# Linear attention with chained states: the products with the states split from their evacuation, and the order of a pair of heads changed

## The chip, the cores and the metric

The kernel runs on one core of a Trainium2 chip. A core has five engines with a queue each, and each queue is worked off in order: TensorE (PE, with its weight loads as PEld) multiplies matrices into PSUM, ScalarE (ACT) and VectorE (DVE) take results out of PSUM and do the elementwise work, GpSimd (POOL) and SyncE (SP) do little here but issue transfers. The metric is the device time of one execution in microseconds. A program says which data an instruction needs; semaphores make the queues wait for each other.

## The reference, cut to what matters

The trunk has two layers over 512 tokens of 1024 features: latent attention and a squared-ReLU MLP, then gated linear attention (GLA) and another MLP. The change is in the GLA mixer, which has four heads with keys of 128 and values of 256.

```
h = xn @ w_in                      # q, k: 512 columns each; v, g: 1024 each; a: 16
gk = log_sigmoid(a @ w_gk_up + b_gk) / 16
b = cumsum(gk) within a chunk
o = (q * exp(b)) @ state + (decayed q k^T, lower triangle) @ v
state = state * exp(b_last) + (k * exp(b_last - b))^T @ v
o = rms_norm(o, g_norm) * silu(g)
out = o @ w_o
```

The kernel cuts the 512 tokens into 4 tiles of 128. Within a tile it builds the decayed scores by halving levels. Between tiles it uses three chained states: state i sums what tiles 0 to i leave to tile i+1, and tile i+1 adds its decayed queries times state i.

## The kernel before, in words

All weights are float32. A product is made of three matmuls over a high and a low part of each operand (`mm3`, lines 110 to 114; `add`, line 1326, for the attention of a head). A weight piece is loaded by SP, then cut by ACT into `wh` (line 104) and by DVE into `wl` (line 107), with three buffers of each.

`gla` has a main stream, `proj()`, and a side stream, `heads()`. `proj()` makes, in this order, the values of heads 0 and 1 ("v"), their gates ("g"), the queries and the keys of heads 2 and 3 ("q", "k"), the values ("V") and the gates ("G") of heads 2 and 3. Each of v, g, V, G is 96 matmuls of 512 columns and counts 8 units; q and k count 4 units each, 48 matmuls each. So a unit is 12 matmuls, and there are 40: v is 1 to 8, g 9 to 16, q 17 to 20 (handed out in twos), k 21 to 24, V 25 to 32, G 33 to 40. After every unit the side stream is let on by 1.27 steps (`PACE`); what it has not done after unit 40 follows behind. The scheduler takes, on each engine, the instruction that stands earliest in this program order among those that are ready, and so keeps this order but for small shifts.

The side stream does heads 0 and 1, then 2 and 3. For a pair of heads it has these steps:

- twelve steps of levels, six for each head, the last of which (`turned`) cuts the decayed queries into `qd` and turns the keys (`kth`, `ktl`); a thirteenth ends the last head's (`late`).
- `states(h)`: nine matmuls of 256 columns for the three sums over a tile (PSUM tag `c`), then their chain on ACT (lines 1319 and 104) and DVE (lines 1315 and 107) into three tiles `S`. There are three buffers of `S` in all, so the next head's `S` can be written only when `past` of the head before has read its own.
- `own_tiles(h)`: twelve matmuls of a head's own scores (`ADh`, `ADl`) times its values. They open the head's two PSUM banks: tags `bb`, `bc`, `aa`, `bb` for heads 0 to 3. The projections of values and gates hold all three `b` banks, so head 3 can have its banks only when G is over; head 2 has the `a` banks, which G does not use.
- `past(h)`: nine matmuls of the queries (`qd`) times `S`, added to the same banks. In the same function stand the squares (ACT, line 1344) and the products with the gates (DVE, line 1346), which empty the banks; these need the gates after their silu (line 1053), so the step comes after `gdone`.
- `gates(2)` and `gates(3)` (once, between the first pair's): the forget gates of heads 2 and 3, from one matmul (line 1142) and a chain on ACT and DVE.
- `head_norm(h)`, and `gather(h)`: the norm, then transposes (line 129) and the cut into `Y` (lines 1365, 1366) for the output projection.

After the second pair's `head_norm`, `out_start` makes 24 matmuls of the output projection with the first pair's `Y`, ahead of the second pair's `gather`; `out_proj` goes on from there. The silu needs its own table of ACT: it is loaded before the four silus of a gate half and the exp and ln table after them.

Of the kernel before, what the change touches and what calls it, by code (L numbers as in the profile page):

```python
# [20 lines left out]
S = 512  # L21
NT = S // P
# [28 lines left out]
def trunk_kernel(ctx: ExitStack, tc: tile.TileContext, t_in: dict, out: bass.AP, out_row: bass.AP):  # L51
# [7 lines left out]
    def uname(s):  # L59
        count[0] += 1  # L60
        return f"{s}_{count[0]}"
# [14 lines left out]
    def bank(tag):  # L76
        return psum["pool"].tile([P, 512], F32, tag=f"ps_{tag}", bufs=psum["banks"][tag], name=uname("ps"))
# [11 lines left out]
    def tmp(shape=(P, 512), dt=F32):  # L89
        return sb.tile(list(shape), dt, tag="tmp", bufs=6, name=uname("tmp"))  # L90
# [30 lines left out]
    def act_e(*a, **k):  # L121
        with tc.issue_after(table[0].ins):
            return ACT.activation(*a, **k)
# [19 lines left out]
    def cut(pair, *idx):  # L143
        return tuple(t[idx] for t in pair)
# [56 lines left out]
    def gcol(name, j):  # L201
        c = GAIN_COL[name] + j
        return gains[:, c : c + 1]
# [559 lines left out]
    def out_start(w2d, X, n):  # L763
        raw = col_chunk(w2d, 0, 256)
        w = [piece(raw[:, :, j * P : (j + 1) * P], ND, P) for j in range(2)]
        ps_ = [bank("a"), bank("a")]

        def mms(ks):
            for k in ks:
                for j in range(2):  # L770
                    mm3(ps_[j], cut(w[j], slice(None), k), X[k], k == 0, k == ND - 1)

        mms(range(n))
        return ps_, lambda: mms(range(n, ND))
# [233 lines left out]
    def gla(layer, nrm, vtag, ytag):  # L1008
# [114 lines left out]
        vdone, gdone = set(), set()  # L1123
# [16 lines left out]
        def gates(h):  # L1140
            p = bank("c")
            PE.matmul(p, wg[:, h * P : (h + 1) * P], av, start=True, stop=True)
            bcol = gcol("bgk", 4 * layer + h)
            l = tmp()
            ACT.activation(l, p, AF.Abs, bias=bcol)
            m_ = tmp()
            DVE.tensor_scalar(m_, p, bcol, 0.0, ALU.add, ALU.min)
            act_e(l, l, AF.Exp, scale=-1.0)
            act_e(l, l, AF.Ln, bias=one_t)

            T = gp.tile([P, 2 * S], F32, tag="T", bufs=3, name=uname("T"))
            DVE.tensor_tensor(T[:, :S], m_, l, ALU.subtract)
            n = S
            c = 0
            D_ = {}
            while n >= 4:
                D_[S // n] = T[:, c : c + n]
                if n > 4:
                    pair_ = T[:, c : c + n].rearrange("p (n a) -> p n a", a=2)
                    DVE.tensor_tensor(T[:, c + n : c + n + n // 2], pair_[:, :, 0], pair_[:, :, 1], ALU.add)  # L1160
                c += n
                n //= 2
            act_e(T[:, :c], T[:, :c], AF.Exp, scale=GSCALE)
            B[h] = D_
# [5 lines left out]
        AT = {}  # L1170
# [131 lines left out]
        def tile_of(pair, i):  # L1302
            return cut(pair, slice(None), slice(i * P, (i + 1) * P))
# [20 lines left out]
        def add(h, i, w, x, start, stop):  # L1324
            for n, (a, b_) in enumerate(((w[0], x[0]), (w[0], x[1]), (w[1], x[0]))):
                PE.matmul(AT[h]["o"][i], a, b_, start=start and n == 0, stop=stop and n == 2, skip_group_check=True)  # L1326
# [6 lines left out]
                add(h, i, at[(i, i)], v[i], i % 2 == 0, i == 0)  # L1333

        def past(h):
            at, hf = AT[h], h // 2
            at["ms"] = sb.tile([P, NT], F32, tag="gms", bufs=2, name=uname("gms"))
            for i in range(NT):
                if i:
                    add(h, i, tile_of(at["q"], i - 1), at["S"][i - 1], False, True)  # L1340
                if i % 2:
                    for r in (i - 1, i):
                        sq = tmp((P, HV))
                        ACT.activation(sq, at["o"][r], AF.Square, accum_out=at["ms"][:, r : r + 1])
                        g = G[hf][:, r, h % 2, :]
                        DVE.tensor_tensor(g, at["o"][r], g, ALU.mult)
# [36 lines left out]
        def heads():  # L1383
            for h in (0, 2):
                while any(i not in qk for i in (h, h + 1, 4 + h, 5 + h)):
                    yield
                late = None
                for two in zip(levels(h), levels(h + 1)):
                    for stage in two:
                        products = stage()  # L1390
                        if late:
                            late()
                        late = products
                        yield
                late()
                yield
                while h // 2 not in vdone:
                    yield

                def run(*stages):  # L1400
                    for stage, r in stages:
                        stage(r)
                        yield

                yield from run((states, h), (own_tiles, h), (states, h + 1))
                while h // 2 not in gdone:
                    yield
                yield from run((own_tiles, h + 1), (past, h))
                if h == 0:
                    gates(2)  # L1410
                yield from run((past, h + 1))
                if h == 0:
                    gates(3)
                yield from run((head_norm, h), (head_norm, h + 1))
                if h:
                    begun.append(out_start(w_o, Y, 4))
                yield from run((gather, h), (gather, h + 1))
# [3 lines left out]
        for _ in rest:  # L1421
            pass
        gates(1)
        main, side = proj(), heads()
        pace = 0.0
        for units in main:
# [194 lines left out]
```

## Time and profile before

| | |
|---|---|
| median of 3 runs | 1086.43 us (1085.32 to 1087.2) |
| the profiled execution, its own time | 1086.99 us |
| its span, first to last instruction | 1085.2 us |
| mean granted TensorE clock | 0.996 |
| PE busy | 1075.3 us |
| DVE, ACT busy | 862.5 us, 555.5 us |

The GLA mixer's side stream lies between about 541 and 706 us of the span, the gate half G between 662 and 688 us with the work put into it. A timeline row gives the start in the span, the time taken, engine, line, operation, the names written and read, shapes, and how many instructions are merged in the row; a bracket at its end gives idle time of the engine before it and what ended that. A matmul's time has its pipeline in it; the distance between the starts of two tells what it costs in a row of many. A row of the stretches gives length of the stretch and, for each engine, busy time and count of instructions, then the granted clock and the DMA's share.

### The profile page before, as it was taken

How to read it: one execution, taken by the hardware profiler on the slowest of the kernel's cores; microseconds unless marked ns; L12 is line 12 of the kernel's file. 1: busy time of each engine (PE TensorE's matmuls, PEld its weight loads, DVE VectorE, ACT ScalarE, POOL GpSimd, SP SyncE). 2: the span in 40 equal slices, each digit the busy share in tenths (PEclk: the TensorE clock that was granted, in tenths of full speed). 3: DMA queues.
4: the chain of work that ended last, by engine and by line, in shares of the span. 5: the costliest groups of instructions: out<-in, count | busy, mean ns of one | idle time of the engine just before them, and what ended most of it. 6: DMA issues, size and time to landing. Idle time of an engine off the chain costs nothing.

```text
span 1085.2 us, 14051 instructions
## 1 busy us (share of the span) xinstructions
PE 1075.3 (99%) x5352; PEld 907.6 (84%) x5352; DVE 862.5 (79%) x1446; ACT 555.5 (51%) x947; POOL 43.7 (4%) x72
## 2 busy tenths in 40 slices
PE   9999999999999999999999999999999999999997
PEld 7888888888888888888788888788888888888886
DVE  7899968987887887977696596469888797797885
ACT  7767654553453453455346655656445345344454
POOL 8310002000000000000000000000000000000000
PEclk9999999999999999999999999999999999999999
DMA  7311232142332332322322213142233234223222
GB/s 225 88 50 39 79 116 78 58 137 78 117 117 78 117 117 78 107 88 79 89 76 78 78 40 117 40 152 66 93 117 117 78 92 131 89 80 124 70 97 78
DMA packets 86195, 101.61 MB, mean 94 GB/s; under 512 B 7440, under 2 KB 64016, under 8 KB 86128
## 3 DMA queue, kind: packets, MB, share of 16 engines
q1 hardware_dynamic: 84320, 99.67, 29.0%
q10 hardware_dynamic: 1808, 1.05, 0.3%
q8 instruction: 42, 0.69, 0.3%
q14 instruction: 25, 0.20, 0.1%
HBM read 98.35 MB, written 2.10 MB: 93 GB/s over the span
## 4 chain that ended last, share of the span: by engine, by line
PE 97%; DVE 1%; ACT 1%; issue 0%; DMA 0%; SPq 0%; ACTq 0%; DVEq 0%
PE ps L114 21%; PE ps L112 21%; PE ps L113 21%; PE ps L923 17%; PE ps L924 9%; PE ps L1199 1%; PE ps L129 1%; PE ps L408 1%; PE ps L871 1%; PE ps L1326 1%; PE ps L671 0%; PE ps L667 0%; PE ps L1249 0%; PE ps L670 0%; PE ps L669 0%
## 5 line engine op out<-in xcount | busy, mean ns | idle before, releaser
L112 PE MATMUL ps<-set,wh 128*128 128x512 f32 x760 | 297.5, 392 | 0.0
L113 PE MATMUL ps<-set,wh 128*128 128x512 f32 x760 | 297.3, 391 | 0.0
L114 PE MATMUL ps<-set,wl 128*128 128x512 f32 x760 | 297.0, 391 | 0.0
L104 ACT ACTIVATE wh<-wraw 128x1024 fp32r<-128x1024 f32 x139 | 147.0, 1061 | 229.1 <-PE ps L113 116.0
L107 DVE TENSOR_TENSOR wl<-wraw,wh 128x1024 fp32r<-128x1024 f32 x139 | 169.4, 1219 | 48.4 <-ACT wh L104 48.2
L114 PEld LDWEIGHTS ps<-set,wl 128*128 128x128 f32 x760 | 143.1, 188 | 30.2
L112 PEld LDWEIGHTS ps<-set,wh 128*128 128x128 f32 x760 | 142.9, 188 | 30.1
L113 PEld LDWEIGHTS ps<-set,wh 128*128 128x128 f32 x760 | 143.2, 188 | 27.6
L923 PE MATMUL ps<-T,wh 128*128 128x512 f32 x448 | 157.5, 391 | 0.0
L924 PE MATMUL ps<-T,wl 128*128 128x256 f32 x448 | 126.2, 282 | 0.0
L923 PE MATMUL ps<-set,wh 128*128 128x512 f32 x336 | 119.9, 397 | 0.0
L923 PEld LDWEIGHTS ps<-T,wh 128*128 128x128 f32 x448 | 84.1, 188 | 18.2
L924 PE MATMUL ps<-set,wl 128*128 128x256 f32 x336 | 94.2, 280 | 0.0
L107 DVE TENSOR_TENSOR wl<-comb,wh 128x1024 fp32r<-128x1024 f32 x42 | 51.3, 1222 | 46.2 <-ACT wh L104 46.0
L104 ACT ACTIVATE wh<-comb 128x1024 fp32r<-128x1024 f32 x42 | 44.6, 1061 | 83.3 <-PE ps L923 81.8
L837 DVE TENSOR_TENSOR xT<-ps,xT 128x512 f32<-128x512 f32 x120 | 82.1, 685 | 6.1 <-PE ps L114 6.1
L924 PEld LDWEIGHTS ps<-T,wl 128*128 128x128 f32 x448 | 84.6, 189 | 0.5
L923 PEld LDWEIGHTS ps<-set,wh 128*128 128x128 f32 x336 | 63.1, 188 | 15.1
L941 DVE TENSOR_TENSOR tmp<-ps,tmp 128x512 f32<-128x512 f32 x98 | 67.1, 685 | 0.9
L924 PEld LDWEIGHTS ps<-set,wl 128*128 128x128 f32 x336 | 63.4, 189 | 1.6
L104 ACT ACTIVATE wh<-raw 128x1024 fp32r<-128x1024 f32 x28 | 29.5, 1054 | 56.7 <-PE ps L923 55.8
L112 PE MATMUL ps<-wh,set 128*128 128x512 f32 x144 | 57.9, 402 | 0.0
(372 smaller groups left out, 1662.8 us busy)
## 6 DMA issues: line engine op xcount, KB each, us to landing
wraw<-in_mlp_w_up_dram SPq DMA_DIRECT2D x32, 1024.0 KB, 5.4
wraw<-in_mlp_w_down_dram SPq DMA_DIRECT2D x18, 1024.0 KB, 5.1
raw<-in_mlp_w_down_dram SPq DMA_DIRECT2D x14, 1024.0 KB, 5.1
wraw<-in_gla_w_in_dram SPq DMA_DIRECT2D x12, 1024.0 KB, 5.2
wraw<-in_mla_w_o_dram SPq DMA_DIRECT2D x4, 1024.0 KB, 5.4
wraw<-in_gla_w_o_dram SPq DMA_DIRECT2D x4, 1024.0 KB, 5.3
xT<-in_x_dram SPq DMA_DIRECT2D x6, 256.0 KB, 5.5
wraw<-in_mla_w_in_dram SPq DMA_DIRECT2D x3, 512.0 KB, 6.6
```

What stands on the lines that cost most here:

```text
L104: order(ACT.activation(hi, src, AF.Copy))
L107: lo_eng.tensor_tensor(lo, src, f(hi), ALU.subtract)
L112: PE.matmul(psum, wh, xh, start=start, stop=False)
L113: PE.matmul(psum, wh, xl, start=False, stop=False)
L114: PE.matmul(psum, wl, xh, start=False, stop=stop)
L129: PE.transpose(psum, src, ident[: src.shape[0], : src.shape[0]])
L408: PE.matmul(p, w[:, i, j * P : (j + 1) * P], x, start=start, stop=stop)
L837: DVE.tensor_tensor(xT[m], p, xT[m], ALU.add)
L871: PE.matmul(ps_[c], a, b_, start=False, stop=k == 3 and n == 2, skip_group_check=True)
L923: PE.matmul(o.rearrange("p (h t) -> p h t", h=2), wh, x, start=start and k == 0, stop=False, skip_group_check=True)
L924: PE.matmul(o[:, :TH], wl, x[:, 0], start=False, stop=k == KH - 1, skip_group_check=True)
L941: DVE.tensor_tensor(by_tile(r), high, by_tile(r), ALU.add)
```

## The change

`past` is cut into two functions: `past(h)` keeps the nine matmuls with the states, and `gated(h)` has the squares and the products with the gates. The order of the steps is written out for each pair.

For heads 0 and 1 the wait for the gates moves ahead of `states(0)`; after it come `states(0)`, `own_tiles(0)`, `states(1)`, `own_tiles(1)`, `past(0)`, `gated(0)`, then `gates(2)`, `past(1)`, `gated(1)`, and `gates(3)`. For heads 2 and 3, `past(2)` stands ahead of `states(3)` and both ahead of the wait for the gates; after the wait come `gated(2)`, `own_tiles(3)`, `past(3)`, `gated(3)`. Each pair has two steps more.

```diff
         def past(h):
+            at = AT[h]
+            for i in range(1, NT):
+                add(h, i, tile_of(at["q"], i - 1), at["S"][i - 1], False, True)
+
+        def gated(h):
             at, hf = AT[h], h // 2
             at["ms"] = sb.tile([P, NT], F32, tag="gms", bufs=2, name=uname("gms"))
             for i in range(NT):
-                if i:
-                    add(h, i, tile_of(at["q"], i - 1), at["S"][i - 1], False, True)
                 if i % 2:
                     for r in (i - 1, i):
                         sq = tmp((P, HV))
...
-                yield from run((states, h), (own_tiles, h), (states, h + 1))
-                while h // 2 not in gdone:
-                    yield
-                yield from run((own_tiles, h + 1), (past, h))
                 if h == 0:
+                    while 0 not in gdone:
+                        yield
+                    yield from run((states, 0), (own_tiles, 0), (states, 1), (own_tiles, 1), (past, 0), (gated, 0))
                     gates(2)
-                yield from run((past, h + 1))
-                if h == 0:
+                    yield from run((past, 1), (gated, 1))
                     gates(3)
+                else:
+                    yield from run((states, 2), (own_tiles, 2), (past, 2), (states, 3))
+                    while 1 not in gdone:
+                        yield
+                    yield from run((gated, 2), (own_tiles, 3), (past, 3), (gated, 3))
                 yield from run((head_norm, h), (head_norm, h + 1))
```

## The prediction, made before the changed kernel was run

> **What bounds the kernel now.** I began with the page: busy times, the granted clock, the chain that ended last.
>
> ```profile
> span 1085.2 us, 14051 instructions
> ...
> PE 1075.3 (99%) x5352; PEld 907.6 (84%) x5352; DVE 862.5 (79%) x1446; ACT 555.5 (51%) x947; POOL 43.7 (4%) x72
> ...
> PE 97%; DVE 1%; ACT 1%; issue 0%; DMA 0%; SPq 0%; ACTq 0%; DVEq 0%
> ```
>
> TensorE is the bound, and the change adds or removes no matmul. It can win only what PE loses by waiting or by a low clock, and lose only by making new waits. So the second view is who PE waited for, over the whole span; the two rows that have to do with the change are these (total, times, longest, in us).
>
> ```profile
> PE ps L1326 <- ACT S L104: 1.0, 2, 0.7
> PE ps L1326 <- DVE S L107: 0.5, 1, 0.5
> ```
>
> L1326 is `add`, so PE waits for state tiles `S` to be cut. The third view cuts the end of the GLA mixer into stretches (length, then PE, PEld, DVE, ACT, POOL busy, then the clock).
>
> ```profile
> 629.00:662.00 33.00, 33.00 (x173) 28.57 (x172) 30.80 (x75) 18.23 (x36) 0.00 (x0) 1.00 0.29 94
> 662.00:675.00 13.00, 13.00 (x74) 11.31 (x73) 6.38 (x11) 5.43 (x10) 0.00 (x0) 1.00 0.19 61
> 675.00:687.70 12.70, 12.70 (x57) 10.51 (x57) 2.45 (x2) 5.36 (x6) 0.00 (x0) 1.00 0.19 64
> 687.70:695.30 7.60, 5.91 (x34) 4.51 (x33) 4.13 (x9) 5.89 (x16) 0.00 (x0) 1.00 0.22 78
> 695.30:698.70 3.40, 3.40 (x10) 2.63 (x9) 2.95 (x12) 3.24 (x16) 0.00 (x0) 0.50 0.01 2
> ```
>
> Two things show. PE is full until 687.7, is busy for 5.91 of the next 7.60 us, and then runs at clock 0.50 for 3.4 us. And DVE is full (30.80 of 33) while the levels of heads 2 and 3 run, but idles afterwards. The fourth view is PE's timeline there.
>
> ```profile
> 665.30 0.32 PE L112 MATMUL ps<-set,kth 128*128 128x256 f32 x1
> ...
> 668.91 0.40 PE L1326 MATMUL ps<-set,ADh 128*128 128x256 f32 x2
> ...
> 670.33 0.28 PE L112 MATMUL ps<-set,kth 128*128 128x256 f32 x1
> ...
> 671.40 0.40 PE L112 MATMUL ps<-wh,set 128*128 128x512 f32 x1
> ...
> 687.74 0.40 PE L1326 MATMUL ps<-set,ADh 128*128 128x256 f32 x2
> ...
> 689.16 2.18 PE L1326 MATMUL ps<-S,qd 128*128 128x256 f32 x12
> 692.02 0.38 PE L1326 MATMUL ps<-S,qd 128*128 128x256 f32 x1 [0.69 <-ACT S L104]
> 692.92 0.50 PE L1326 MATMUL ps<-S,qd 128*128 128x256 f32 x2 [0.51 <-DVE S L107]
> 693.76 0.96 PE L1326 MATMUL ps<-S,qd 128*128 128x256 f32 x3 [0.34 <-ACT S L104]
> 694.58 0.50 PE L112 MATMUL ps<-set,wh 128*128 128x512 f32 x1
> ...
> 695.42 0.63 PE L112 MATMUL ps<-set,wh 128*128 128x512 f32 x1
> ...
> 698.79 0.39 PE L114 MATMUL ps<-set,wl 128*128 128x512 f32 x1
> ...
> 701.77 1.47 PE L129 MATMUL ps<-ident,g 128*128 128x128 f32 x12
> 703.14 0.73 PE L112 MATMUL ps<-set,wh 128*128 128x512 f32 x2
> ```
>
> Read it with the steps. 665.30 is `states(2)`, 668.91 `own_tiles(2)`, 670.33 `states(3)`, all inside the gate half G; 671.40 to 687.74 are G's last 72 matmuls, 0.227 us each. Then `own_tiles(3)`, 12 matmuls in 1.42 us (0.118 each), and from 689.16 the 18 of `past(2)` and `past(3)`. Though the products of `states(3)` were done by 671.40, their `S` are cut only now, since the three buffers of `S` are held by head 2 until `past(2)`, which stood behind G. ACT's timeline shows what that chain meets:
>
> ```profile
> 687.94 0.69 ACT L1053 ACTIVATE g<-ps,rtok 128x512 f32<-128x512 f32 x1 [0.68 <-PE ps L114]
> 688.65 1.28 ACT L119 ACT_TABLE_LOAD   x1
> 689.94 0.38 ACT L104 ACTIVATE S<-ps 128x256 fp32r<-128x256 f32 x1
> 690.22 1.05 ACT L104 ACTIVATE wh<-wraw 128x1024 fp32r<-128x1024 f32 x1
> ```
>
> The last silu and the table load hold the first cut up to 689.94, and a weight cut of 1.05 us gets in between.
>
> **The change, part by part.**
>
> *Where the steps land.* The side stream gets 1.27 steps a unit. Before, the end of the levels (`late`) is step 40, in unit 32; `states(2)` is 41 (unit 33), `own_tiles(2)` and `states(3)` 42 and 43 (unit 34); then it waits for unit 40. The trace agrees: `states(2)` comes after G's first unit. After the change heads 0 and 1 wait until unit 16 with `states(0)` (step 20, it was 14) and each pair has two steps more. Counting on: `past(0)`, `gated(0)` 24 and 25 (unit 20), `gates(2)` with `past(1)` 26 (unit 22), `gates(3)` 28 (unit 24), levels of heads 2 and 3 steps 32 to 43 (units 26 to 34), `late` 44 (35), `states(2)` 45 (36), `own_tiles(2)` 46 (37), `past(2)` and `states(3)` 47 and 48 (both unit 38), wait in 39, `gated(2)` in 40. Behind G stand `own_tiles(3)`, `past(3)`, `gated(3)`.
>
> *`past(2)` inside G.* Nine matmuls of 0.118, 1.06 us, move ahead of G's end; G ends at 687.74 + 1.06 = 688.80. That costs nothing in sum. Does it find its `S`? The chain of head 2 runs in G already:
>
> ```profile
> 666.25 0.48 ACT L1319 ACTIVATE tmp<-ps,D 128x256 f32<-128x256 f32 x1 [2.03 <-PE ps L114]
> ```
> ```profile
> 665.09 0.55 DVE L107 TENSOR_TENSOR ktl<-ps,kth 128x384 fp32r<-128x384 f32 x1
> ...
> 669.27 0.42 DVE L107 TENSOR_TENSOR S<-tmp,S 128x256 fp32r<-128x256 f32 x1 [0.15 <-ACT S L104]
> ```
>
> From 665.30, the start of the products, to 669.69 are 4.4 us. Between `states(2)` and `past(2)` will lie its own 9 matmuls (1.1), two units (24 x 0.227 = 5.4) and `own_tiles(2)` (1.4): 7.9 us. So no wait.
>
> *`states(3)` cut inside G.* Its `S` are free as soon as `past(2)` has read. After its products come units 39 and 40 (5.4 us) and `own_tiles(3)` (1.4 us), 6.8 us in all, against the chain's 4.4 - 1.1 = 3.3 us behind the products. ACT's silus fall into this stretch; the chain may have to let by a table load (1.28) and two silus (2 x 0.69), which makes 6.0 us. It still fits by 0.8 us. So the 18 matmuls from 689.16 to 694.58, 5.42 us where 18 x 0.118 = 2.13 would do, lose their wait: **-3.29 us**. (The brackets show only 1.54 us of it, since the modelled ends of matmuls count as busy.)
>
> *The clock.* The eight matmuls from 695.42 to 698.79 take 3.37 us, and at 0.227 would take 1.81. The low clock begins 0.7 us after the wait ends, and while PE has work there is no other drop in the span (stretches as above):
>
> ```profile
> 6.00:687.70 681.70, 681.19 (x3380) 573.60 (x3379) 545.79 (x971) 363.04 (x634) 41.70 (x62) 1.00 0.29 91
> ...
> 698.70:1081.00 382.30, 380.13 (x1914) 322.54 (x1913) 307.16 (x440) 179.87 (x281) 0.00 (x0) 1.00 0.30 97
> ```
>
> I take it as the wait's doing: **-1.56 us**. [...]
>
> *What is late next.* Behind G, PE has `own_tiles(3)` 1.42, `past(3)` 1.06 and the 24 matmuls of `out_start` (5.45), so it comes to `gather(2)` at 688.80 + 7.93 = 696.7 instead of 701.77, and, eight transposes of 1.37 / 12 = 0.114 later, to `gather(3)` at 697.6. The norm chain has to keep up:
>
> ```profile
> 696.25 0.38 ACT L1344 ACTIVATE tmp<-ps 128x256 f32<-128x256 f32 x1
> ...
> 696.63 0.38 ACT L1344 ACTIVATE tmp<-ps 128x256 f32<-128x256 f32 x1
> ...
> 698.07 0.19 ACT L1344 ACTIVATION_READ_ACCUMULATOR tmp<-ps 128x1 f32 x1
> ...
> 699.48 0.91 ACT L1353 ACTIVATE g<-g,srstd 128x256 f32<-128x256 f32 x2 [0.66 <-DVE srstd L285]
> ```
>
> ACT's last silu ends 0.89 us after G (688.63 - 687.74), the table load 1.28 later, at 691.0. Eight squares at 0.38 bring 694.0, the weight cut 1.05 more, 695.1; from the last square (698.26) to the last scaling (700.39) it took 2.13, so 697.2. It is in time by 0.4 us even if no square of head 2 is done earlier. This cover is thin; without it the cost is what ACT is late by, at most 1 us.
>
> *Heads 0 and 1 later.* `states(0)`, `own_tiles(0)` and `states(1)` leave the first gate half and go between q and k, which are PE work that is always at hand. `past(0)` comes two units behind, longer than the chain of 4.4 us. `past(1)` stands two units (5.4 us) behind `past(0)`, which frees its `S`: 3.3 us are needed. I cost both at nothing.
>
> *Levels of heads 2 and 3 later.* `gates(3)` moves from unit 20 to 24 (10.9 us), the levels' end from unit 32 to 35, `states(3)` from 34 to 38 (10.9 us and `past(2)`). Head 3's keys were cut at 665.64, 4.7 us before their use; that slack stays. DVE's full stretch will reach some 9 us into G, where it is idle for 6.6 of 13 and 10.2 of 12.7 us. The emptying of V's banks, which G's first matmuls need, then stands among level work. No row shows that; between nothing (no gain, for PE has no wait there to lose) and 1.5 us (some two of the longest single wait, 0.69), I take +0.35, nearer to nothing, as PE did not wait once from 629 to 687.7 under a full DVE.
>
> *Queues.* No moved step issues a transfer; SP's loads come from the main stream, whose order stays. POOL has nothing here. The added wait for the first gates holds back steps of the program, not an engine.
>
> *Sum.* -3.29 - 1.56 + 0.35 = -4.5 us. The profiled execution took 1086.99 (span 1085.2 and 1.8 around it), so it would take 1082.5; the median of the runs stands 0.56 lower, at 1086.43, which gives **1081.9 us**.
>
> **The rivals.**
>
> 1. *A unit late.* The full DVE holds head 2's keys for a unit or two, so `states(3)` runs right before G's end and its chain meets four silus and two table loads. For: the slack is 0.8 us. Against: before, the steps were on time by G. With one unit between them, the chain ends 3.3 + 2.66 - 2.7 = 3.3 us behind G, and `past(3)` would begin at 1.42: some 1.8 us of the wait stay, 1083.7.
> 2. *The clock drops all the same*, at another place or with the waits that are left. For: gaps of 0.3 to 0.7 us only brought it about, and small ones will remain. Against: it is the only drop, right behind the wait. Then 1086.43 - 3.29 + 0.35 = 1083.5.
> 3. *The change doesn't do what it says*: the chain of `states(3)` is put behind the silus on ACT, as now. Then `past(3)` waits as now, while `past(2)` no longer helps to cover it (1.06 us): between 1086.4 and 1087.5.
> 4. *Slower.* The late start of heads 0 and 1 pushes the levels through the stretch where DVE has no room, and `states(2)` falls behind G. It decides when the keys of head 2 come over four units and the work between, some 15 us, later than planned. Then two chains stand open, each of 4.4 us, less the 3.9 us of products that can go first (1.1 + 1.42 + 1.42): a stall of about 4.9 us instead of 3.29, and another window of low clock: 1088.0 to 1089.6. The same sign would come from `past(1)` or V's first matmuls waiting for head 1's banks.
>
> **How the numbers follow.** The forecast has 0.55, rival 1 0.11, rival 2 0.08, rival 3 0.09, rival 4 and its kin 0.17. The first three make faster 0.74; a change within 0.2% (2.2 us, about what a measurement of this kernel can tell from none) 0.09; slower 0.17. The range starts at 1080.8, the full -4.85 with some 0.8 for small waits on the chain behind the gather, and ends at 1086.6, which takes in rival 3's lower end and leaves out rival 4.
>
> **What would show it.** In the changed profile nine matmuls `ps<-S,qd` stand inside G, before `states(3)`; no wait of L1326 for `S` is left near 690; the clock stays 1.00 from 687 to 700; G's end is some 1 us later and the first transposes of the second pair come about 4 us earlier, without a wait for `g`. It is wrong if `S` cuts still stand behind the table load at L119, if DVE's late levels show as waits of PE for banks at the change from V to G, or if PE waits between q and k.

## The result, and the profile after

The changed kernel takes 1084.27 us (median of 8 runs, 1083.29 to 1084.92); the kernel before, run beside it, 1087.0 us (median of 8, 1085.32 to 1088.36). The ratio is 0.9974, with a 95% interval of 0.9963 to 0.9984. So 2.7 us are won (1.7 to 4.0 by the interval) where 4.5 were forecast. The profiled execution took 1084.2 us with a span of 1082.2 us, against 1086.99 and 1085.2.

The page of the changed kernel, its first lines and the shares of the chain that ended last:

```profile
span 1082.2 us, 14050 instructions
...
PE 1072.8 (99%) x5352; PEld 906.4 (84%) x5352; DVE 864.5 (80%) x1446; ACT 556.2 (51%) x947; POOL 43.7 (4%) x72
...
PE 96%; DVE 2%; ACT 1%; DMA 0%; issue 0%; SPq 0%; DVEq 0%; ACTq 0%
```

PE has the same 5352 matmuls. DVE's share of the chain has gone from 1% to 2%, but a rounded per cent is some 11 us of the span and tells nothing of a wait of one. The view of waits for PE (total, times, longest, in us) no longer has a row of L1326; two rows of this stretch are new:

```profile
PE ps L112 <- DVE g L1349: 0.8, 1, 0.8
PE ps L112 <- ACT set L1368: 0.2, 1, 0.2
```

The stretches (length, then PE, PEld, DVE, ACT, POOL busy, then the clock) answer to those of before:

```profile
662.00:675.00 13.00, 13.00 (x70) 11.07 (x70) 8.24 (x12) 8.82 (x19) 0.00 (x0) 1.00 0.50 163
675.00:689.00 14.00, 14.00 (x77) 12.14 (x76) 5.20 (x10) 7.34 (x15) 0.00 (x0) 1.00 0.23 76
689.00:692.60 3.60, 2.75 (x23) 2.51 (x21) 1.65 (x5) 3.57 (x10) 0.00 (x0) 1.00 0.00 0
692.60:698.10 5.50, 5.50 (x24) 4.48 (x25) 4.54 (x15) 4.36 (x17) 0.00 (x0) 1.00 0.01 1
```

The clock is 1.00 throughout. DVE was busy for 6.38 of 13 us from 662 to 675 and is now busy for 8.24: the levels have moved into G, as worked out. In these stretches PE is full but for one place between 689.0 and 692.6, and there ACT is full (3.57 of 3.60). PE's timeline:

```profile
681.46 1.22 PE L1326 MATMUL ps<-S,qd 128*128 128x256 f32 x9
682.51 0.28 PE L112 MATMUL ps<-set,kth 128*128 128x256 f32 x1
...
683.58 0.39 PE L112 MATMUL ps<-wh,set 128*128 128x512 f32 x1
...
689.03 0.40 PE L1326 MATMUL ps<-set,ADh 128*128 128x256 f32 x2
...
690.45 1.22 PE L1326 MATMUL ps<-S,qd 128*128 128x256 f32 x9
692.52 0.51 PE L112 MATMUL ps<-set,wh 128*128 128x512 f32 x1 [0.85 <-DVE g L1349]
...
698.11 1.70 PE L129 MATMUL ps<-ident,g 128*128 128x128 f32 x12
700.05 0.73 PE L112 MATMUL ps<-set,wh 128*128 128x512 f32 x2 [0.25 <-ACT set L1368]
```

`past(2)` (681.46) stands inside G, without a wait, and `states(3)` (682.51) behind it. G's last 24 matmuls run from 683.58 to 689.03, then come `own_tiles(3)` and `past(3)` (690.45), nine matmuls in one row, no `S` late. Then there is a hole that the prediction does not have. The last of the nine starts at 690.45 + 8 x 0.118 = 691.39 and the first matmul of `out_start` only at 692.52: 1.13 us from start to start instead of 0.12, so 1.0 us is lost. And the twelve transposes from 698.11 take 1.94 us until PE goes on at 700.05, where before they took 1.37.

Why PE waits for a product with the gates (L1349) is on ACT's and DVE's timelines:

```profile
688.55 0.73 ACT L104 ACTIVATE S<-tmp 128x256 fp32r<-128x256 f32 x2
689.16 0.39 ACT L1347 ACTIVATE tmp<-ps 128x256 f32<-128x256 f32 x1
...
689.52 0.71 ACT L1053 ACTIVATE g<-ps,rtok 128x512 f32<-128x512 f32 x1
690.24 1.28 ACT L119 ACT_TABLE_LOAD   x1
691.53 0.38 ACT L1347 ACTIVATE tmp<-ps 128x256 f32<-128x256 f32 x1
...
695.28 0.38 ACT L1347 ACTIVATE tmp<-ps 128x256 f32<-128x256 f32 x1 [0.81 <-DVE g L1349]
...
698.52 0.91 ACT L1356 ACTIVATE g<-g,srstd 128x256 f32<-128x256 f32 x2 [0.66 <-DVE srstd L285]
```
```profile
689.68 0.42 DVE L1349 TENSOR_TENSOR g<-ps,g 128x256 f32<-128x256 f32 x1
692.04 0.79 DVE L1349 TENSOR_TENSOR g<-ps,g 128x256 f32<-128x256 f32 x2 [1.94 <-ACT tmp L1347]
693.36 1.23 DVE L107 TENSOR_TENSOR wl<-wraw,wh 128x1024 fp32r<-128x1024 f32 x1 [0.52 <-ACT wh L104]
```

`out_start` writes into the two `a` banks. Those are head 2's, and its squares (L1347) and products (L1349) have to empty them first. A bank holds two of head 2's tiles. The first square is at 689.16, behind the last cuts of `S` (688.55); the second is behind the fourth silu and the table load, at 691.53; the second product follows at 692.04 and PE at 692.52.

### The profile page after: what moved, and what is told of

The parts are those of the page before. It is cut to its first block, busy times and chain, and to the rows that moved or that the text cites. A ratio compares the mean times of both kernels' runs of the same rounds, so it can differ in the third digit from the quotient of the medians.

```text
span 1082.2 us, 14050 instructions
## 1 busy us (share of the span) xinstructions
PE 1072.8 (99%) x5352; PEld 906.4 (84%) x5352; DVE 864.5 (80%) x1446; ACT 556.2 (51%) x947; POOL 43.7 (4%) x72
## 3 DMA queue, kind: packets, MB, share of 16 engines
q10 hardware_dynamic: 1808, 1.05, 0.3%
## 4 chain that ended last, share of the span: by engine, by line
PE 96%; DVE 2%; ACT 1%; DMA 0%; issue 0%; SPq 0%; DVEq 0%; ACTq 0%
PE ps L114 20%; PE ps L112 20%; PE ps L113 20%; PE ps L923 17%; PE ps L924 9%; PE ps L1199 2%; PE ps L129 1%; PE ps L408 1%; PE ps L871 1%; PE ps L1326 1%; PE ps L1249 0%; PE ps L671 0%; PE ps L667 0%; PE ps L670 0%; PE ps L669 0%; DMA gains<-in_gains_dram 0%
```

## The experiments

The variants were run in three groups, each on one chip beside the kernel before, whose medians were 1086.7, 1086.92 and 1086.78 us; each ratio is to the kernel before of its own group, and is not exactly the quotient of two medians. Edits are shown against the changed kernel, those of s_spare and busy_wait against the kernel before. The start of a span, in which the first inputs arrive, differs by up to 1.6 us between profiles: the first matmul of L664 after 80 us of span starts between 83.5 and 85.1 us, though nothing is changed up to there. For the question of where time goes I therefore also give distances from that matmul, which in the kernel before and in the changed one starts at

```profile
L664 PE MATMUL ps<-kf,qf x2: 273/274/275, 84.1 to 84.2; 128*128 128x128 f32 x2
```
```profile
L664 PE MATMUL ps<-kf,qf x2: 275/275/275, 84.1 to 84.3; 128*128 128x128 f32 x2
```

(rows of one line's instructions: shortest, median and longest in ns, first and last start). The table's distances, in us, run from it to the start of `own_tiles(3)` (G's end), to the first matmul of `out_start`, to the second pair's first transpose and to the end of the span; median and ratio are those of the runs.

| kernel | median | ratio, 95% | G's end | out_start | transposes | end |
|---|---|---|---|---|---|---|
| before | 1087.0 | | 603.64 | 610.48 | 617.66 | 1001.13 |
| changed | 1084.27 | 0.9974 (0.9963 to 0.9984) | 604.89 | 608.38 | 613.97 | 998.04 |
| first_pair | 1086.68 | 0.9996 (0.9987 to 1.0005) | 603.78 | 610.64 | 617.83 | 1001.34 |
| second_pair | 1082.53 | 0.9966 (0.9953 to 0.9978) | 604.73 | 607.21 | 612.81 | 996.89 |
| s_spare | 1083.77 | 0.9975 (0.9965 to 0.9984) | 603.65 | 608.92 | 614.52 | 997.99 |
| squares_early | 1083.87 | 0.9975 (0.9965 to 0.9984) | 604.84 | 608.65 | 614.23 | 998.02 |
| busy_wait | 1085.53 | 0.9987 (0.9978 to 0.9995) | 603.64 | 610.49 | 616.11 | 999.62 |
| other_bank | 1083.12 | 0.9962 (0.9949 to 0.9974) | 604.85 | 607.33 | 612.79 | 996.99 |
| squares_first | 1082.35 | 0.9956 (0.9942 to 0.9969) | 604.86 | 607.34 | 612.79 | 996.75 |
| second_squares | 1082.41 | 0.9957 (0.9944 to 0.9969) | 604.76 | 607.24 | 612.69 | 996.53 |

### One pair's order at a time

first_pair has the new order for heads 0 and 1 only (in it and in second_pair, `whole(h)` is `past(h)` and then `gated(h)`):

```diff
-                    yield from run((states, 2), (own_tiles, 2), (past, 2), (states, 3))
+                    yield from run((states, 2), (own_tiles, 2), (states, 3))
...
-                    yield from run((gated, 2), (own_tiles, 3), (past, 3), (gated, 3))
+                    yield from run((own_tiles, 3), (whole, 2), (whole, 3))
```

> The order of the first pair as after the change, that of the second pair as before, squares and products with the gates again right behind each past. My theory: nothing is won, the 18 matmuls with S still take 5.4 us and the clock still falls to 0.5 behind them; the time is that of before within 0.7 us, at most 0.3 us over it for a G that ends later. Rival, that the first pair's order has a share in the gain: faster than before by over 0.7 us.

It measured 1086.68 us beside 1086.7 of before. Nothing is won, and the wait and the low clock are those of before; its rows of the timeline and of the stretches:

```profile
691.68 0.38 PE L1326 MATMUL ps<-S,qd 128*128 128x256 f32 x1 [0.69 <-ACT S L104]
692.57 0.50 PE L1326 MATMUL ps<-S,qd 128*128 128x256 f32 x2 [0.51 <-DVE S L107]
```
```profile
691.03:694.45 3.42, 1.83 (x7) 1.16 (x8) 3.19 (x7) 2.10 (x9) 0.00 (x0) 1.00 0.01 2
694.45:697.86 3.41, 3.41 (x9) 2.64 (x9) 2.66 (x11) 3.16 (x14) 0.00 (x0) 0.50 0.00 0
```

second_pair has the new order for heads 2 and 3 only:

```diff
-                    while 0 not in gdone:
-                        yield
-                    yield from run((states, 0), (own_tiles, 0), (states, 1), (own_tiles, 1), (past, 0), (gated, 0))
+                    yield from run((states, 0), (own_tiles, 0), (states, 1))
+                    while 0 not in gdone:
+                        yield
+                    yield from run((own_tiles, 1), (whole, 0))
                     gates(2)
-                    yield from run((past, 1), (gated, 1))
+                    yield from run((whole, 1))
```

> The order of the first pair as before, that of the second pair as after the change. My theory: the whole gain comes from the second pair, where the S of head 3 are cut inside G; this gives the time of the changed kernel again, 2.8 us under before (0.9974) within 0.5 us, no wait of L1326 for S, no low clock near 695, and still the wait of some 1.0 us ahead of out_start's first matmul. Rival: the later start of the first pair is part of it (it makes room for the levels, or it costs 0.2 us at G's end); then this is slower than the changed kernel by over 0.5 us, or faster by 0.2.

It measured 1082.53 us, better than the whole change. PE comes from `past(3)` to `out_start` without a hole, and one square of head 2 is already done at 678.34, next to the cuts of `S`:

```profile
691.28 1.23 PE L1326 MATMUL ps<-S,qd 128*128 128x256 f32 x9
692.34 0.39 PE L112 MATMUL ps<-set,wh 128*128 128x512 f32 x1
```
```profile
678.34 0.37 ACT L1347 ACTIVATE tmp<-ps 128x256 f32<-128x256 f32 x1
...
678.70 0.41 ACT L104 ACTIVATE S<-tmp 128x256 fp32r<-128x256 f32 x1
```

So the new order of the first pair costs 1.15 us (998.04 less 996.89) and gives nothing. Its steps push those of heads 2 and 3 some 8 us later (`states(3)` begins at 682.51 - 84.14 = 598.4 there and at 675.15 - 85.13 = 590.0 here, counted from the same matmul), and with them the cuts of head 3's `S`: the last of them stands at 678.70 here and behind three silus, at 688.55, in the changed kernel, with the first square behind it. Two kernels further down bear this out: with head 2's squares put ahead of these cuts, the first pair's new order costs only 0.22 us (996.75 of squares_first less 996.53 of second_squares), so most of its price goes through the place of the squares.

### The cause of the old wait

s_spare is the kernel before with head 3's `S` in buffers of another tag; no step is moved:

```diff
-                parts = gp.tile([P, 2, HV], F32R, tag="S", bufs=3, name=uname("S"))
+                parts = tmp((P, 2, HV), F32R) if h == 3 else gp.tile([P, 2, HV], F32R, tag="S", bufs=3, name=uname("S"))
```

> The kernel before with no step moved, only the three S tiles of head 3 in buffers of the tag tmp instead of S, so that they need not wait for past(2). My theory (the three buffers of S are the cause of the wait): the S of head 3 are cut inside G, the 18 matmuls with S take 2.1 to 2.4 us instead of 5.4, the clock stays up, out_start then waits about 1 us for the banks of head 2; 2.5 to 3.5 us faster than before. Rival (the wait comes from ACT's table load and silus whatever the buffers): the wait stays over 2 us and the time within 1 us of before.

It measured 1083.77 us. The nine matmuls of `past(3)` go through in one row, and the wait has moved behind them:

```profile
690.06 1.23 PE L1326 MATMUL ps<-tmp,qd 128*128 128x256 f32 x9
692.86 0.49 PE L112 MATMUL ps<-set,wh 128*128 128x512 f32 x1 [1.57 <-DVE g L1346]
```

The three buffers of `S` were the cause, as read from the profile. And here, too, the next thing late is the emptying of head 2's banks, by more than the 1 us expected (1.57 in the bracket). Buffers alone win as much as the new order.

### The cause of the new wait

squares_early is the changed kernel with head 2's four squares issued behind `states(3)`, ahead of the wait for the gates; `weighed` has the products alone:

```diff
-                    yield from run((states, 2), (own_tiles, 2), (past, 2), (states, 3))
+                    yield from run((states, 2), (own_tiles, 2), (past, 2), (states_squares, 3))
...
-                    yield from run((gated, 2), (own_tiles, 3), (past, 3), (gated, 3))
+                    yield from run((weighed, 2), (own_tiles, 3), (past, 3), (gated, 3))
```

> The changed kernel with the four squares of head 2 issued behind the products of states(3), inside G, and only its products with the gates behind the wait. My theory (out_start waits for the banks of head 2, which the squares keep back behind the last silu and the table load, and the same squares hold up the norm before the transposes): the wait of 1.0 us before out_start falls to under 0.3, the 12 transposes take 1.4 instead of 1.9 us, and the time is 1.0 to 1.6 us under the changed kernel, some 4.0 us under before. Rival (the products with the gates or head 3's chain hold as long): within 0.4 us of the changed kernel.

It measured 1083.87 us: a miss. The squares are issued earlier in the program, but behind `states(3)`, and on ACT the first two stand where they stood (the product that PE waits for is L1362 here):

```profile
689.04 0.73 ACT L104 ACTIVATE S<-tmp 128x256 fp32r<-128x256 f32 x2
689.65 0.39 ACT L1357 ACTIVATE tmp<-ps 128x256 f32<-128x256 f32 x1
...
690.72 1.28 ACT L119 ACT_TABLE_LOAD   x1
692.02 0.38 ACT L1357 ACTIVATE tmp<-ps 128x256 f32<-128x256 f32 x1
```
```profile
693.33 0.50 PE L112 MATMUL ps<-set,wh 128*128 128x512 f32 x1 [1.16 <-DVE g L1362]
```

Either the place on ACT was still wrong, or the squares were not the cause. ACT was idle between the cuts of `S` while the squares could have run, 0.82 us ahead of 685.49; why the order left those gaps empty was not found out. The next two kernels decide between the two. squares_first has the same squares one step earlier, behind `past(2)` and ahead of `states(3)`:

```diff
-                    yield from run((states, 2), (own_tiles, 2), (past, 2), (states, 3))
+                    yield from run((states, 2), (own_tiles, 2), (past_squares, 2), (states, 3))
...
-                    yield from run((gated, 2), (own_tiles, 3), (past, 3), (gated, 3))
+                    yield from run((weighed, 2), (own_tiles, 3), (past, 3), (gated, 3))
```

> The changed kernel, with head 2's four squares issued right behind past(2), ahead of states(3), and only the products with the gates behind the wait. Theory 'what was late in the changed kernel and in the one with the squares behind states(3) is the place of the second square on ACT, behind the last state cuts, the fourth silu and the table load': four squares at about 683 to 685 us, the products behind the silus, no wait in front of the output projection (1.0 us), no wait at the transposes (0.5 us), 1082.4 us; up to 0.8 us of it is lost if the state tiles of head 3, whose chain stands behind the squares, come late to past(3): 1083.1. Rival 'the start of the output projection waits for something else': nothing changes, 1083.9.

It measured 1082.35 us. Its four squares run from 683.33 on, its products come behind each silu (the last is done at 691.08), and the hole in front of `out_start` is gone:

```profile
683.33 0.36 ACT L1357 ACTIVATE tmp<-ps 128x256 f32<-128x256 f32 x1
...
684.39 0.39 ACT L1357 ACTIVATE tmp<-ps 128x256 f32<-128x256 f32 x1
```
```profile
691.16 1.23 PE L1326 MATMUL ps<-S,qd 128*128 128x256 f32 x9
692.22 0.39 PE L112 MATMUL ps<-set,wh 128*128 128x512 f32 x1
...
697.67 1.61 PE L129 MATMUL ps<-ident,g 128*128 128x128 f32 x12
699.52 0.73 PE L112 MATMUL ps<-set,wh 128*128 128x512 f32 x2 [0.24 <-ACT set L1381]
```

The part of the expectation on the transposes did not come true: they still take 1.85 us (697.67 to 699.52).

other_bank leaves the squares alone and gives PE another bank: the first half of `out_start` goes into the third `b` bank, with its twelve matmuls first.

```diff
-        ps_ = [bank("a"), bank("a")]
+        ps_ = [bank(tag) for tag in tags]
...
-                    begun.append(out_start(w_o, Y, 4))
+                    begun.append(out_start(w_o, Y, 4, "ba"))
```

> The changed kernel, with the first half of the output projection's start in the third b bank, which has been free since the gates' last silu, all twelve matmuls of that half first, and the second half in an a bank. Theory 'PE waits for head 2's banks to be emptied': the 1.0 us in front of the first of these matmuls is gone, PE comes to the second pair's transposes about 1 us earlier, and most of it is lost there again, since the last scaling of g is ready only at about 699.4 us: 1083.5 to 1083.9 for 1083.9 of the changed kernel. Rival 'PE waits there for something else' (the gathered first pair or the cut weights): the wait stays in front of the first matmul of the output projection, 1083.9 to 1084.2.

It measured 1083.12 us, a larger gain than expected: the hole is gone, and little was lost at the transposes (0.13 us, 1.18 at their start less 1.05 at the end), where PE did eight of them, then matmuls of the output projection, then the other eight:

```profile
690.54 1.22 PE L1331 MATMUL ps<-S,qd 128*128 128x256 f32 x9
691.61 0.39 PE L112 MATMUL ps<-set,wh 128*128 128x512 f32 x1
```

The bank is what PE waited for; with squares_first that is shown from both sides.

second_squares joins the two good halves, the second pair's order alone and the squares ahead of `states(3)`; its edit to second_pair is that of squares_first.

> The first pair in its old order, the second in the new one, and head 2's squares right behind past(2), ahead of states(3). Theory 'all that is left is ACT's queue behind the table load': the 0.45 us in front of the second pair's transposes goes, 1082.0 to 1082.2 for the 1082.5 without the early squares. Rival 'the transposes wait for the bank or the norm chain of head 3 alone': no change, 1082.5. With PE without a wait in this stretch, no further gain is to be had from these steps.

It measured 1082.41 us, nearer to the rival. By the distances 0.36 us are won against second_pair (996.89 and 996.53), and from the transposes to the end it still takes 383.84 us, where before it was 383.47: the wait there is smaller, not gone. With no other wait of PE in the stretch the kernel comes out 4.6 us below before (1001.13 less 996.53), about what was forecast.

### The changed kernel and squares_first on one chip

> The changed kernel itself once more, to stand beside the variants. Both theories expect its own level again, 1083.9 to 1084.4 us, 2.6 to 2.9 us below the kernel before; if it comes out at 1082.5, the variants with the early squares or the old first pair gained nothing, and the wait in front of the output projection is covered by something else.

> The kernel with head 2's squares right behind past(2) once more, on the same chip as the changed kernel. If the wait in front of the output projection is the loss against the prediction, it stays 1.2 to 1.9 us below the changed kernel, at 1082.3 to 1082.8; if the two differ by less than 0.6 us, the earlier difference lay between the chips.

The changed kernel measured 1084.27 us (ratio to before 0.9975, 0.9966 to 0.9984), squares_first 1082.25 us (0.9959, 0.9946 to 0.9971). The difference between the two medians is 2.0 us, just over the range expected. Between the two profiled executions the distances show 1.25 us (997.98 and 996.73 to the end), and 0.76 lies ahead of the first matmul of L664, which the edit does not touch. That part differs between two profiles of squares_first itself (84.88 and 83.55 us), and is not explained.

### The cause of the low clock

busy_wait is the kernel before with ten matmuls into a spare bank, put among `past(3)`; nobody reads them:

```diff
+                if h == 3 and i:
+                    if i == 1:
+                        idle = bank("c")
+                    for _ in range((0, 7, 3, 0)[i]):
+                        PE.matmul(idle, ones_r, X[0][0], start=True, stop=True)
```

> The kernel before, with ten matmuls of 512 columns added between the groups of past(3), seven behind the first state tile's and three behind the second's; nobody reads their result, and the attention's own matmuls still wait for the state tiles. PE then has work during the wait (10 x 0.227 = 2.3 us of the 2.8 us by which the starts of the 18 matmuls stand too far apart). Theory 'the low clock comes from PE's idle time': no stretch at 0.50 near 695 us, the wait stays, and the median falls by the 1.2 to 1.6 us that the stretch cost, to 1085.1 to 1085.5. [...]

It measured 1085.53 us beside 1086.92, a ratio of 0.9987 (0.9978 to 0.9995), with the matmuls added. `out_start` begins at the same distance as before (610.49 and 610.48), so the wait is still there; but there is no stretch at 0.50, and the transposes come 1.55 us earlier (616.11 and 617.66). The rows of the stretches, from `past(2)` on:

```profile
689.30:694.80 5.50, 5.42 (x30) 4.14 (x30) 3.83 (x9) 4.39 (x12) 0.00 (x0) 1.00 0.02 7
694.80:700.40 5.60, 5.60 (x26) 4.54 (x25) 4.47 (x18) 4.42 (x18) 0.00 (x0) 1.00 0.00 1
```

The other executions agree: the mean granted clock is 0.998 or 0.999 in all eleven executions with the added matmuls, and 0.995 to 0.999 in the fifteen of the kernel before beside them. So, by this run, PE's idle time in the wait is what brought the clock down.

## Why the prediction was right in direction and off in size

**Where the steps land: right.** `states(2)` has 48 of G's matmuls behind it and so comes after unit 36, `own_tiles(2)` 36 (unit 37), `past(2)` and `states(3)` 24 (unit 38), as counted.

**`past(2)` and the cuts inside G: right.** No matmul of L1326 waits for `S`. The chain of head 3 ends 6.2 us behind its products (the last row of `S` on DVE, 689.00 and 0.76 long, against 683.58), where 6.0 were forecast. From the end of G to `out_start` PE needed 6.84 us before (610.48 less 603.64) and needs 2.48 in squares_first; 1.06 of the difference is `past(2)`, which moved, and 3.30 the wait, forecast at 3.29.

**The clock: right, and shown.** The forecast was -1.56; between `out_start` and the transposes the changed kernel is 1.59 faster (7.18 and 5.59), and busy_wait won 1.55 there alone, 1.4 in the medians. The second rival falls: the clock stays at 1.00 in the profile, and its mean is 0.998 or 0.999 in every execution of the changed kernel.

**Heads 0 and 1 later, costed at nothing: wrong.** Nothing of the first pair waits, but its steps delay the second pair's, and that brings head 3's cuts of `S` among the silus. I looked only at whether the cuts come in time for `past(3)`, where they had 0.8 us to spare, and not at what stands behind them on ACT. second_pair shows the price: 1.15 us.

**What is late next: the step that failed.** I let PE go from `past(3)` straight on to `out_start` and did not ask whose banks it writes to. They are head 2's, and their emptying hangs on the tail that I had worked out for the norm: silu, table load, squares. I held that tail against the transposes of `gather(3)` at 697.6, where it seemed in time by 0.4 us, and not against the product of the second square, which PE needed by 691.3 (688.80 + 1.42 + 1.06). That is 1.0 us. For the transposes I took eight squares in a row at 0.38 us. In the trace a square waits for the product before it (695.28, 0.81 us for DVE), and DVE has a weight cut of 1.23 us in between, so the scaling that I put at 697.2 ended at 699.4 (698.52 + 0.91). The square at 695.28 starts 0.03 us after the two products at 694.50 end (0.75 us for both); what kept it from running beside them, no run shows. PE came to the transposes at 698.11 instead of 696.7 and needed 1.94 us for the first twelve, 0.57 more than before; I had named that cost, at up to 1 us, and left it out. This part is read from the timelines, and no run isolates it: the early squares of second_squares took 0.24 of the 0.6 us away (384.08 us from the transposes to the end in second_pair, 383.84 there).

**Levels later, +0.35: near in size, by luck.** G ends at 689.03 instead of 688.80, and by the distances 0.19 us later than `past(2)` explains (604.89 less 603.64 less 1.06). But the wait that I priced, for V's banks at the change from V to G, is not there. Up to G's end first_pair is 0.14 us behind the kernel before (603.78 and 603.64), so the time goes with the first pair's order; where PE loses it was not found.

**The sum.** From the start of the first transposes before (701.77) to that after (698.11) are 3.66 us, less some 0.6 behind them, 3.1 in the distances (1001.13 less 998.04). The forecast had 4.85 less an allowance of 0.35. The losses that this allowance should have held are 0.23 at G's end, 1.0 in front of `out_start`, 0.6 at the transposes: 1.8 us. By its number alone the result lies nearer to the first two rivals (1083.7 and 1083.5) than to the forecast, but neither occurred, and nor did the third: no matmul waits for `S`, and the clock stays up. (The first rival's price, which I worked out wrongly, counts one table load and two silus, 2.66 us, where its condition names two and four.) Of the fourth, only the cause did, the late start of heads 0 and 1, and it cost 1.15 us by another way than the one described.

## What to carry to other kernels

When a wait is taken away, ask of the work that then comes first not only whether its inputs are ready, but also whose buffers or banks it writes into and what chain empties them. An engine that is idle on average (ACT is busy for 556.2 of 1082.2 us) can still be the bound in a tail (3.57 of 3.60 us): put its instructions in queue order, with table loads (1.28 us here) and waits for another engine (0.81 us at the square at 695.28), and compare each one with the moment at which it is needed. If a step gives nothing itself, as the first pair's new order here, look at what it makes late in the queue behind it; leaving it out won 1.15 us.

## What the runs showed of the clock

The low stretch near 695 us lasted 3.41 us in the kernel before and in first_pair (rows here and above) and did not need a long gap: before, the three gaps are 0.34 to 0.69 us, and in the changed kernel one gap of 0.85 us did nothing. What differs between the cases shown here is how much work PE had in the 3.41 us ahead. In the trace of the kernel before the record of the clock begins with 1.00 at 5.83 us of the span and changes at 695.32, 698.73 and 1081.02, which is 202, 203 and 315 times 3.413 us later; in that of the changed kernel it begins at 6.57 and changes at 1078.35, 314 times later. The stretches compared here are laid on that step, counted from where the record of their trace begins. I give the work as an estimate: 0.227 us for each matmul of 512 columns that starts in a stretch and 0.118 for each of 256, their distances in full rows. The kernel before has 3 of 512 and 6 of 256, 1.39 us, in the stretch that the low clock follows (first_pair, above, 1 and 6, 0.93 us):

```profile
691.90:695.32 3.42, 2.37 (x9) 1.62 (x10) 2.78 (x7) 1.98 (x11) 0.00 (x0) 1.00 0.00 0
695.32:698.73 3.41, 3.41 (x9) 2.64 (x9) 2.98 (x12) 3.25 (x15) 0.00 (x0) 0.50 0.01 2
```

s_spare, with the longest single gap of all (1.57 us), has 3 and 8, 1.62 us, in its emptiest stretch here, and keeps its clock:

```profile
690.12:693.53 3.41, 1.84 (x13) 1.55 (x13) 2.32 (x4) 2.18 (x9) 0.00 (x0) 1.00 0.01 2
693.53:696.94 3.41, 3.41 (x17) 2.78 (x16) 2.89 (x12) 3.19 (x16) 0.00 (x0) 1.00 0.00 0
```

(The busy times don't show it, since modelled ends count as busy, and the counts of these rows also take in matmuls that only reach into the stretch.) The number of matmuls does not tell these cases apart: 7 start in first_pair's stretch above, which the low clock follows, and near its end it has one with no more than 7 either, but all of 512 columns, 1.59 us, behind which the clock stays at 1.00 for 3.42 us more, without a matmul:

```profile
1076.74:1080.15 3.41, 1.84 (x9) 1.17 (x7) 1.12 (x4) 1.19 (x4) 0.00 (x0) 1.00 0.39 154
1080.15:1083.57 3.42, 0.00 (x0) 0.00 (x0) 1.00 (x3) 0.51 (x1) 0.00 (x0) 1.00 0.40 153
```

So in these rows the clock is at 0.50 behind 1.39 and 0.93 us of work and at 1.00 behind 1.62 and 1.59 us. That the work in such a stretch decides is my estimate from these four; no run was made to test it.

The mean clock is not the same in every execution. The 23 executions of the kernel before in the first group have a mean granted clock of 0.995 to 0.999, and their times go with it: 1084.9 to 1085.3 us at 0.999, 1087.6 to 1088.1 at 0.995. The term of 1.56 us is thus that of one profile, not of every execution, and what made the executions differ was not shown. In that profile three short gaps were followed by a loss of 1.56 us, about half of the 3.30 us of the wait itself.
